# Two sums of quarters on GpSimd at each change of the resident operand, and row sums of the mixing's weights in fp32r

## The chip, the cores and the metric

The kernel runs on one core of a Trainium2 chip. The metric is its device time in microseconds; lower is better. TensorE (PE, with its weight loads as PEld) multiplies matrices, VectorE (DVE), ScalarE (ACT) and GpSimd (POOL) work on elements, and SyncE (SP) issues most of the DMAs. Operands lie in SBUF, products are accumulated in PSUM.

## The reference, cut to what matters

The program is one layer of a gated block over 1024 positions of 1024 channels, in fp32: a normalised input is projected into many parts; a windowed attention and a spatial gating are multiplied by gates and projected, and the two are added with further gates and projected once more.

```python
proj = h @ w_in[l]
q, k, v, za, u, vs, zs, gm = jnp.split(proj, IN_SPLITS, axis=-1)
...
a = (a * jax.nn.silu(za)) @ w_att_out[l]
sgo = chunked_spatial_gating(...)
sgo = (sgo * jax.nn.silu(zs)) @ w_sg_out[l]
ga, gs = jnp.split(jax.nn.sigmoid(gm + b_merge[l]), N_BRANCHES, axis=-1)
y = ga * a + gs * sgo
x = x + y @ w_o[l]
```

The spatial gating normalises `vs` over its channels with a scale `ln_g` and an offset `ln_b`, and mixes the 128 positions of a block by a masked 128 x 128 matrix per group of channels:

```python
v = layernorm(v, ln_g, ln_b)
...
mixed = jnp.einsum('gij,bnjgc->bnigc', w, vb) + jnp.transpose(b_s)[None, None, :, :, None]
return u * mixed.reshape(B, S, SG_WIDTH)
```

Since the offset is the same at all positions, it enters the mixed value as `ln_b` times the sum of a row of the mixing matrix. These are the row sums of the change.

## The kernel before, in words

**Products.** Every large product runs transposed, with one operand resident in SBUF (`b`) and the weights streaming past it. It is done by Strassen's scheme in Winograd's form: both operands are cut into quarters, and seven products of sums of quarters take the place of eight. The seven forms of the resident operand are `b11, t1, t2, b21, t3, b22, t4` (FORMS): b11, b21 and b22 are quarters themselves, t1 = q12 - q11 up to sign, t2 = t1 and q22 together, t3 = q11 combined with that, and t4 = q21 combined with it. Each of them lies in one buffer (tiles `T_b11h`, `T_b11l` and so on), so the form of a new operand can be written only after the old operand's last product has read it.

**Two halves of a number.** An fp32 number is split (`split`, L145 to 154) into a rounded high part, a cast on ScalarE (L153), and the rest, a subtraction on VectorE (L154). A product (`product`, L339) then is three passes (high by high, high by low, low by high) over four blocks of 128: 12 matmuls of 128 x 512. Weights are split likewise into `wh` and `wl`, each with three buffers of 128 x 1024; `split_next` does the next unit. `gemm_pair` runs the seven products of a pair of blocks of weights, and joins them by VectorE operations with one operand in PSUM (L369, L374, L378); its `finish` applies what follows, and sends the result to DRAM.

**Changes of the resident operand.** Two stages change it while the last pair of the stage before still runs: `s_forms` ahead of the projection of the gating branch (about 670 to 710 us) and `a_forms` ahead of that of the attention (about 746 to 790 us). `forms_of` gets the four quarters in `bq` tiles (128 x 2048 fp32, in halves of 128 x 1024), and forms sums in place by `combine` (L181 to 183, two instructions each): q12 := q11 - q12, then q12 := q22 + q12, then q11 := q12 - q11, and last q21 := q12 - q21. Between them each form is split into its tiles by `fill`. What leaves the pairs meanwhile is put into `a_dr` (L455, first change) and `y_dr` (second change) by DMAs that GpSimd issues.

**The mixing.** The second half of the projection `vs` runs as an ordinary gemm with eight PSUM banks as accumulators (L564, results into `xh` by L695 on ScalarE). Then the pairs of `u` begin. Their hooks run the statistics, the normalisation (L737), and, at the first and third pair (m = 0 and 4), `bias_of`: it loads a bias, makes the row sums of four groups of the mixing's weights `mix_w` (tile `wT`) by one fp32 matmul with a tile of `ones` (L747) into a bank `sc`, and combines the three on VectorE. `mix` uses these afterwards (L767). The `sc` banks have no other use in that stage.

**Order.** The instructions of an engine run in the order in which a scheduler put them when the program was built, and an instruction waits for the semaphores of what it reads and overwrites; so an instruction that moves in the source, or to another engine, also moves others against each other on the engines' queues.

Of the kernel before, what the change touches and what calls it, by code (L numbers as in the profile page):

```python
# [24 lines left out]
F32 = mybir.dt.float32  # L25
F32R = mybir.dt.float32r
AF = mybir.ActivationFunctionType
ALU = mybir.AluOpType
PSUM = bass.MemoryType.PSUM

P = 128
D = 1024
S = 1024
KC = D // P
# [18 lines left out]
def hybrid_tile(  # L53
# [16 lines left out]
    nc = tc.nc  # L70
# [8 lines left out]
    def nm(s):  # L79
        count[0] += 1  # L80
        return f"{s}_{count[0]}"

    def bank(tag, dt=F32):
        return psum.tile([P, 512], dt, name=nm("ps_" + tag), tag="ps_" + tag, bufs=2)

    def mtile(shape, dt, tag, bufs, pool=None):
        return (pool or main).tile(shape, dt, name=nm(tag), tag=tag, bufs=bufs)
# [13 lines left out]
    ident = const.tile([P, P], F32, name="ident")  # L101
# [10 lines left out]
    lb_sb = const.tile([P, KC], F32, name="lb_sb")  # L112
# [33 lines left out]
    def split(hi, lo, src, minus=False):  # L146
        if minus:
            nc.scalar.mul(hi, src, -1.0)
            nc.vector.scalar_tensor_tensor(
                lo, src, -1.0, hi.bitcast(F32), op0=ALU.mult, op1=ALU.subtract  # L150
            )
        else:
            nc.scalar.copy(hi, src)  # L153
            return nc.vector.tensor_sub(lo, src, hi.bitcast(F32))  # L154
# [18 lines left out]
    def new_b(names=FORMS):  # L173
        return {n: (slot(n + "h"), slot(n + "l")) for n in names}

    def fill_b(b, name, src, minus=None):
        hi, lo = b[name]
        for c in range(0, 4, 2):
            split(hi[:, c : c + 2, :], lo[:, c : c + 2, :], src[:, c : c + 2, :], name == "t2" if minus is None else minus)

    def combine(op, dst, a, c):  # L181
        for i in range(0, 4, 2):
            op(dst[:, i : i + 2, :], a[:, i : i + 2, :], c[:, i : i + 2, :])
# [22 lines left out]
    def split_next():  # L206

        if not units:
            begin_job()
        if not units:  # L210
            return
        halves, keys = units.pop(0)
        if keys[0][1] == 2:
            make_sums()
        hi = mtile([P, D], F32R, "wh", 3)
        lo = mtile([P, D], F32R, "wl", 3)
        if isinstance(halves, list):
            for c, half in enumerate(halves):
                split(hi[:, half_of(c)], lo[:, half_of(c)], half)
        else:  # L220
            wide = halves.shape[1]
            first = split(hi[:, 0:wide], lo[:, 0:wide], halves)
            if keys[0] == (done[0] - 1, 6) and done[0] > LAST_OF_Q + 2:
                make_sums(first)
        for c, key in enumerate(keys):
            ready[key] = hi[:, half_of(c)], lo[:, half_of(c)]
        if len(units) == 1:
            begin_job()

    def half_of(half):  # L230
        return slice(half * HALF, (half + 1) * HALF)
# [243 lines left out]

    outer = ExitStack()
    gelu = outer.enter_context(tc.tile_pool(name="gelu", bufs=1))
    head = ExitStack()
    hpool = head.enter_context(tc.tile_pool(name="head", bufs=1))
    xh = mtile([P, NT, D], F32, "xh", 1, gelu)  # L480
    stats = mtile([P, NT, 2, 6], F32, "bn", 1, gelu)
    mv = mtile([P, NT, 2], F32, "mv", 1, gelu)

    def htile(shape, dt, tag):
        return mtile(shape, dt, tag, 1, hpool)

    def load_x(t):
        xt = raw_tile()
# [145 lines left out]
    def gelu_of(t):  # L634
        two = xh[:, t : t + 2, 0:HALF]
        after(nc.scalar.activation(two, two, AF.Gelu), casts[-1])
        for i in range(2):
            statistics(t + i, 0)
# [6 lines left out]
    def make_forms():  # L645
# [29 lines left out]
        for c in range(0, 4, 2):  # L675
            form("t4", last[c // 2][:], c)
            yield

    accs = [bank(tag) for tag in ("mm", "mm", "o", "o", "sc", "sc", "tp", "tp")]
    aside = [lambda t=t: gelu_of(t) for t in range(0, NT, 2)]  # L680
    forms = make_forms()
# [3 lines left out]
    for c in range(4):  # L685
        if c + 2 < 4:
            weights.append(vs_weights(c + 2))
        for t in range(NT):
            wh, wl = weights[c]
# [7 lines left out]
                aside.pop(0)()  # L697
    while aside:
        aside.pop(0)()
    of_head = sinks.rearrange("(c e r) -> e c r", e=2, r=2)  # L700
    for e in range(2):
        nc.sync.dma_start(
# [5 lines left out]
    nc.sync.dma_start(lb_sb[:], ln_b)  # L708
    for _ in range(3):
        split_next()  # L710
    head.close()


    stage = ExitStack()
    stage.enter_context(outer)
    pool = stage.enter_context(tc.tile_pool(name="mixing", bufs=1))
    late = []

    def hook():
        for _ in range(2):  # L720
            if late:
                late.pop(0)()

    mix_w = mtile([P, KC, P], F32, "wT", 1, pool)
    nc.sync.dma_start(mix_w[:], sg_w)
    nc.vector.memset(mix_w[64:128, :, 0:64], 0.0)
    ones = mtile([P, P], F32, "ones", 1, pool)
    nc.gpsimd.memset(ones[:], 1.0)

    def statistics_of(t):  # L730
        statistics(t, 1)
# [9 lines left out]
    def bias_of(half):  # L741

        wT = mix_w[:, half * 4 : half * 4 + 4, :]
        bg = mtile([P, 4, P], F32, "bias", 1, pool)
        nc.sync.dma_start(bg[:].rearrange("p g i -> p (g i)"), sg_b[half_of(half)].partition_broadcast(P))
        rs = bank("sc")
        nc.tensor.matmul(  # L747
            rs[:],
            ones[:],
            wT.rearrange("p g i -> p (g i)"),  # L750
            start=True,
            stop=True,
        )
        for gg in range(4):
            g = half * 4 + gg
            nc.vector.scalar_tensor_tensor(
                bg[:, gg, :], rs[:, gg * P : (gg + 1) * P], lb_sb[:, g : g + 1], bg[:, gg, :], op0=ALU.mult, op1=ALU.add
            )
        return bg, wT

# [31 lines left out]
    for m in range(0, KC, 2):  # L792

        def finish(i, half, q, src, sign, m=m):
            nc.scalar.activation(q[:], src, AF.Gelu, scale=sign)
            late.append(lambda: mix(m + i, half, q))

        if m % 4 == 0:
            late.append(lambda m=m: bias.append(bias_of(m // 4)))
        gemm_pair(hb, finish, both)  # L800
# [5 lines left out]
    stage = ExitStack()  # L806
    pool = stage.enter_context(tc.tile_pool(name="keys", bufs=1))
# [43 lines left out]
    stage = ExitStack()  # L851
    pool = stage.enter_context(tc.tile_pool(name="queries", bufs=1))
# [229 lines left out]
    stage = ExitStack()  # L1082
    pool = stage.enter_context(tc.tile_pool(name="attention", bufs=1))
# [188 lines left out]
    stage = ExitStack()  # L1272
    pool = stage.enter_context(tc.tile_pool(name="later", bufs=1))
# [48 lines left out]
    def forms_of(qs):  # L1322
        q11, q12, q21, q22 = (qs[k] for k in QUARTERS)
        b = {}

        def fill(name, q):
            b.update(new_b((name,)))
            fill_b(b, name, q)

        combine(nc.vector.tensor_sub, q12, q11, q12)  # L1330
        yield
        fill("b11", q11)
        fill("t1", q12)
        combine(nc.vector.tensor_add, q12, q22, q12)
        fill("t2", q12)
        fill("b21", q21)
        combine(nc.vector.tensor_sub, q11, q12, q11)
        fill("t3", q11)
        fill("b22", q22)
        combine(nc.vector.tensor_sub, q21, q12, q21)  # L1340
        fill("t4", q21)
        yield b

# [8 lines left out]
    for m in range(0, KC, 2):  # L1352
        if m == 0:
            want_gates(at_dr, m)
        if m == 2:
            s_q = {}
            ahead_of_time += loads_of_quarters(s_q, s_dr)
        if m == 6:
            s_forms = forms_of(s_q)
            next(s_forms)  # L1360

        def finish(i, half, q, src, sign):
            nc.scalar.activation(q[:], src, AF.Silu, scale=sign)
            nc.vector.tensor_mul(q[:], q[:], gates.pop(0)[:])
            put(a_dr, m + i, half, q[:], nc.gpsimd)
            if m < 6:
                gates.append(get(at_dr, m + 2 + i, half, 4))

        gemm_pair(hb, finish, part_of_loads, "tp")
# [19 lines left out]
    for m in range(0, KC, 2):  # L1389
        if m == 2:  # L1390
            a_q = {}
            ahead_of_time += loads_of_quarters(a_q, a_dr)
        if m == 6:
            a_forms = forms_of(a_q)
            next(a_forms)

        def finish(i, half, q, src, sign):
            gated(q, src, sign, gate_of(gs_dr, m, i, half, KC))
            put(y_dr, m + i, half, q[:], nc.gpsimd)
            gates.append(get(gs_dr, m + 2 + i, half, 4) if m < 6 else get(ga_dr, i, half, 4))  # L1400

        gemm_pair(sb_, finish, part_of_loads, "tp")
# [125 lines left out]
    for p in range(4):  # L1528
        n, t, acc, x11 = N_PAIRS + p, T_ORDER[p], accs[p], firsts[p]
# [173 lines left out]
```

## Time and profile before

| | |
|---|---|
| time, median of 3 runs | 928.03 us (928.03 to 928.74) |
| the profiled execution's own time | 928.07 us |
| its span | 926.3 us |
| granted TensorE clock, mean | 0.997 |
| core | 1 of 1 |

The page gives for each engine the busy time and its share of the span. An instruction's idle time is put down to what released it. In the timeline, a row has the start, the duration, the engine, the line of the kernel, the operation, out<-in by tile names, the shape, and a count where equal neighbours are put together; behind it in brackets the idle time before it with its releaser. Neighbouring instructions of an engine overlap a little, so what an instruction costs its engine is the distance between starts. Matmuls recorded as 0.39 long start every 0.227 us.

### The profile page before, as it was taken

Reading aid. Unit: us, or ns where it says so; the run is one execution under the profiler, and the core shown is the slowest. Engines: PE = TensorE matmul, PEld = TensorE weight load, DVE = VectorE, ACT = ScalarE, POOL = GpSimd, SP = SyncE. Lnnn points to the kernel's source line nnn. Section 1 sums busy time; section 2 is a strip of 40 time slices with the busy share of each in tenths; the row PEclk is TensorE's granted clock in tenths of the full one; section 3 lists DMA queues with packets and bytes.
Section 4 is the critical chain, followed back from the end, with each engine's and each line's share of the span. In section 5 each row is a group of like instructions: output and inputs, shape, how many; then the busy total and the mean of one; then the engine's idle time right before and its main releaser. Section 6 shows DMA issues by size and latency. Waiting matters only on the chain.

```text
span 926.3 us, 13222 instructions
## 1 busy us (share of the span) xinstructions
PE 906.1 (98%) x4337; PEld 751.3 (81%) x4337; DVE 690.2 (75%) x1243; ACT 530.2 (57%) x1056; POOL 126.8 (14%) x189
## 2 busy tenths in 40 slices
PE   8999999999999989999999999999999999999996
PEld 5888888888888778778888888888887887888885
DVE  6874776656678678888878888746498589579996
ACT  7852433334444468887766676744475475467443
POOL 0002222213011001101111121001100111210012
PEclk9999999999999999999999999999999999999998
DMA  7328778887788777778787779779669765998632
GB/s 261 137 89 210 215 195 180 157 161 219 240 286 262 216 242 200 214 212 232 188 228 258 234 168 262 209 263 324 212 197 330 257 196 157 289 316 283 207 114 114
DMA packets 128972, 202.23 MB, mean 218 GB/s; under 512 B 12456, under 2 KB 60840, under 8 KB 128904
## 3 DMA queue, kind: packets, MB, share of 16 engines
q1 hardware_dynamic: 109752, 148.69, 49.1%
q0 software_dynamic: 19008, 52.44, 24.0%
q8 instruction: 34, 0.56, 0.2%
q14 instruction: 34, 0.28, 0.1%
q10 hardware_dynamic: 144, 0.26, 0.1%
HBM read 144.59 MB, written 86.11 MB: 249 GB/s over the span
## 4 chain that ended last, share of the span: by engine, by line
PE 74%; DVE 11%; DMA 7%; ACT 3%; issue 3%; SPq 1%; DVEq 0%; ACTq 0%
PE ps_mm L339 31%; PE ps_o L339 22%; PE ps_mm L595 4%; DVE wl L154 3%; PE ps_sc L339 2%; PE ps_tp L339 2%; PE ps_sc L1110 2%; PE ps_o L1195 2%; PE ps_tp L1154 2%; DMA wr<-in_w_dram 1%; PE ps_tp L564 1%; PE ps_sc L564 1%; PE ps_o L564 1%; PE ps_mm L564 1%; PE ps_tp L767 1%
## 5 line engine op out<-in xcount | busy, mean ns | idle before, releaser
L153 ACT CAST wh<-s 128x1024 fp32r<-128x1024 f32 (+1 forms) x78 | 78.2, 1005 | 95.3 <-PE ps_mm L339 44.7
L154 DVE TENSOR_TENSOR wl<-wr,wh 128x1024 fp32r<-128x1024 f32 (+1 forms) x80 | 75.7, 947 | 56.4 <-ACT wh L153 55.5
L153 ACT CAST wh<-wr 128x1024 fp32r<-128x1024 f32 (+1 forms) x80 | 66.3, 830 | 79.8 <-PE ps_mm L339 37.8
L154 DVE TENSOR_TENSOR wl<-s,wh 128x1024 fp32r<-128x1024 f32 (+1 forms) x78 | 90.9, 1166 | 12.1 <-ACT wh L153 12.1
L339 PE MATMUL ps_o<-T_b22h,wh 128*128 128x512 f32 x148 | 58.8, 398 | 1.7 <-ACT x L361 1.7
L339 PE MATMUL ps_o<-T_t1h,wh 128*128 128x512 f32 x148 | 59.2, 400 | 0.3 <-ACT wh L153 0.2
L339 PE MATMUL ps_o<-T_b22l,wh 128*128 128x512 f32 x148 | 57.8, 391 | 0.0
L339 PE MATMUL ps_o<-T_b22h,wl 128*128 128x512 f32 x148 | 57.8, 390 | 0.0
L339 PE MATMUL ps_o<-T_t1h,wl 128*128 128x512 f32 x148 | 57.7, 390 | 0.0
L339 PE MATMUL ps_o<-T_t1l,wh 128*128 128x512 f32 x148 | 57.7, 390 | 0.0
L339 PE MATMUL ps_mm<-T_b11h,wl 128*128 128x512 f32 x140 | 54.8, 392 | 2.1 <-DVE wl L154 2.1
L339 PE MATMUL ps_mm<-T_t4h,wh 128*128 128x512 f32 x140 | 55.2, 394 | 1.5 <-DVE x L374 0.8
L339 PE MATMUL ps_mm<-T_t2h,wh 128*128 128x512 f32 x140 | 54.9, 392 | 1.3 <-ACT x L357 1.2
L339 PE MATMUL ps_mm<-T_t3h,wh 128*128 128x512 f32 x140 | 55.4, 396 | 0.2 <-ACT x L364 0.2
L1123 ACT ACTIVATE pr<-ps_sc,sm 128x192 f32<-128x192 f32 (+2 forms) x128 | 50.9, 409 | 8.1 <-DVE sm L1119 7.1
L339 PE MATMUL ps_mm<-T_b11h,wh 128*128 128x512 f32 x140 | 55.0, 393 | 0.0
L339 PE MATMUL ps_mm<-T_t4h,wl 128*128 128x512 f32 x140 | 54.7, 391 | 0.0
L339 PE MATMUL ps_mm<-T_t3h,wl 128*128 128x512 f32 x140 | 54.7, 390 | 0.0
L339 PE MATMUL ps_mm<-T_b11l,wh 128*128 128x512 f32 x140 | 54.6, 390 | 0.0
L339 PE MATMUL ps_mm<-T_t2h,wl 128*128 128x512 f32 x140 | 54.6, 390 | 0.0
L339 PE MATMUL ps_mm<-T_t4l,wh 128*128 128x512 f32 x140 | 54.5, 390 | 0.0
L339 PE MATMUL ps_mm<-T_t2l,wh 128*128 128x512 f32 x140 | 54.5, 390 | 0.0
(352 smaller groups left out, 2403.9 us busy)
## 6 DMA issues: line engine op xcount, KB each, us to landing
wr<-in_w_dram SPq DMA_DIRECT2D x86, 256.0 KB
sums<-in_w_dram POOLq DMA_DIRECT2D x20, 512.0 KB, 5.6
s<-sums SPq DMA_DIRECT2D x20, 512.0 KB
s_dr<-x SPq DMA_DIRECT2D x32, 256.0 KB
q_hl<-qhl SPq DMA_DIRECT2D x16, 512.0 KB
q<-q_hl SPq DMA_DIRECT2D x64, 128.0 KB
wr<-in_w_dram SPq DMA_DIRECT2D x14, 512.0 KB
y_dr<-x POOLq DMA_DIRECT2D x28, 256.0 KB, 6.6
```

Source lines behind the costliest of these rows:

```text
L153: nc.scalar.copy(hi, src)
L154: return nc.vector.tensor_sub(lo, src, hi.bitcast(F32))
L339: nc.tensor.matmul(acc, lt, rt, start=fresh and k == 0 and n == 0, stop=k == 3 and n == 2, skip_group_check=True,)
L564: mm = nc.tensor.matmul(acc, lt, rt, start=k == 0 and n == 0, stop=k == KC - 1 and n == 2)
L595: nc.tensor.matmul(acc[:], lt, rt, start=k == 0 and n == 0, stop=k == KC - 1 and n == 2)
L767: nc.tensor.matmul(pm[:, t * P : (t + 1) * P], xh[:, half * 4 + t, g * P : (g + 1) * P], bias[-1][1][:, g % 4, :], start=True, stop=True,)
L1110: nc.tensor.matmul(sc[:, i, k0:], q_of[:, c, i * P : (i + 1) * P], kt[:, f, k0:], start=f == 0, stop=f == 1,)
L1123: nc.scalar.activation(held_in[c, i], sc[:, i, lo:hi], AF.Exp, bias=nmax[:, c, i : i + 1], scale=-1.0, accum_out=sums[:, c, i : i + 1],)
L1154: nc.tensor.transpose(dst, pr[:, i, block * P : block * P + width], ident[:])
L1195: nc.tensor.matmul(po[:, cs], lt, rt, start=n == 0, stop=n == len(terms) - 1)
```

## The change

Both edits leave the results what they were. At each change of the resident operand, the two last sums of quarters (into q11 and into q21, two instructions of 128 x 1024 each) are made by GpSimd instead of VectorE. The row sums are made before the first pair of `u` and no longer inside the first and third: the mixing's weights are loaded and masked, and the ones made, before the second-half gemm of `vs`; the weights are split once into high and low part, in one of the three `wh`/`wl` buffers, and two fp32r matmuls per half, four in all, sum them up directly after the gemm. The two `sc` banks keep the sums until the third pair. The ones are made by VectorE from the identity instead of by a memset on GpSimd.

In the built program the order on the engines changes as follows. On GpSimd, at the first change the two q11 instructions stand ahead of the first of the four `a_dr` issues, and the q21 instructions between the later ones; at the second the q11 instructions stand ahead of the four `y_dr` issues of the last pair and the q21 ones behind them. VectorE's order becomes `T_b21l`, both halves of `T_t3l`, `T_b22l` and `T_t4l`, and then the `wl` of the next pair. On TensorE, the first change had a third to a half of the next pair's first products ahead of the product of t4; now the product of t4 stands first. SyncE issues the load of the mixing's weights behind the fourth load of x. VectorE's and ScalarE's instructions in the first 62 us are put in another order.

```diff
--- before.py
+++ after.py
@@ -475,14 +475,10 @@
 
     outer = ExitStack()
     gelu = outer.enter_context(tc.tile_pool(name="gelu", bufs=1))
-    head = ExitStack()
-    hpool = head.enter_context(tc.tile_pool(name="head", bufs=1))
+    pool = outer.enter_context(tc.tile_pool(name="mixing", bufs=1))
     xh = mtile([P, NT, D], F32, "xh", 1, gelu)
     stats = mtile([P, NT, 2, 6], F32, "bn", 1, gelu)
     mv = mtile([P, NT, 2], F32, "mv", 1, gelu)
-
-    def htile(shape, dt, tag):
-        return mtile(shape, dt, tag, 1, hpool)
 
     def load_x(t):
         xt = raw_tile()
@@ -676,6 +672,11 @@
             form("t4", last[c // 2][:], c)
             yield
 
+    mix_w = mtile([P, KC, P], F32, "wT", 1, pool)
+    nc.sync.dma_start(mix_w[:], sg_w)
+    nc.vector.memset(mix_w[64:128, :, 0:64], 0.0)
+    ones = mtile([P, P], F32R, "ones", 1, pool)
+    nc.vector.tensor_scalar(ones[:], ident[:], 0.0, 1.0, op0=ALU.mult, op1=ALU.add)
     accs = [bank(tag) for tag in ("mm", "mm", "o", "o", "sc", "sc", "tp", "tp")]
     aside = [lambda t=t: gelu_of(t) for t in range(0, NT, 2)]
     forms = make_forms()
@@ -697,6 +698,13 @@
                 aside.pop(0)()
     while aside:
         aside.pop(0)()
+
+    row_sums = [bank("sc") for half in range(2)]
+    wh, wl = mtile([P, D], F32R, "wh", 3), mtile([P, D], F32R, "wl", 3)
+    split(wh[:], wl[:], mix_w[:].rearrange("p g i -> p (g i)"))
+    for half in range(2):
+        for n, part in enumerate((wh, wl)):
+            nc.tensor.matmul(row_sums[half][:], ones[:], part[:, half_of(half)], start=n == 0, stop=n == 1)
     of_head = sinks.rearrange("(c e r) -> e c r", e=2, r=2)
     for e in range(2):
         nc.sync.dma_start(
@@ -708,24 +716,16 @@
     nc.sync.dma_start(lb_sb[:], ln_b)
     for _ in range(3):
         split_next()
-    head.close()
 
 
     stage = ExitStack()
     stage.enter_context(outer)
-    pool = stage.enter_context(tc.tile_pool(name="mixing", bufs=1))
     late = []
 
     def hook():
         for _ in range(2):
             if late:
                 late.pop(0)()
-
-    mix_w = mtile([P, KC, P], F32, "wT", 1, pool)
-    nc.sync.dma_start(mix_w[:], sg_w)
-    nc.vector.memset(mix_w[64:128, :, 0:64], 0.0)
-    ones = mtile([P, P], F32, "ones", 1, pool)
-    nc.gpsimd.memset(ones[:], 1.0)
 
     def statistics_of(t):
         statistics(t, 1)
@@ -743,18 +743,10 @@
         wT = mix_w[:, half * 4 : half * 4 + 4, :]
         bg = mtile([P, 4, P], F32, "bias", 1, pool)
         nc.sync.dma_start(bg[:].rearrange("p g i -> p (g i)"), sg_b[half_of(half)].partition_broadcast(P))
-        rs = bank("sc")
-        nc.tensor.matmul(
-            rs[:],
-            ones[:],
-            wT.rearrange("p g i -> p (g i)"),
-            start=True,
-            stop=True,
-        )
         for gg in range(4):
             g = half * 4 + gg
             nc.vector.scalar_tensor_tensor(
-                bg[:, gg, :], rs[:, gg * P : (gg + 1) * P], lb_sb[:, g : g + 1], bg[:, gg, :], op0=ALU.mult, op1=ALU.add
+                bg[:, gg, :], row_sums[half][:, gg * P : (gg + 1) * P], lb_sb[:, g : g + 1], bg[:, gg, :], op0=ALU.mult, op1=ALU.add
             )
         return bg, wT
 
@@ -1334,10 +1326,11 @@
         combine(nc.vector.tensor_add, q12, q22, q12)
         fill("t2", q12)
         fill("b21", q21)
-        combine(nc.vector.tensor_sub, q11, q12, q11)
+
+        combine(nc.gpsimd.tensor_sub, q11, q12, q11)
         fill("t3", q11)
         fill("b22", q22)
-        combine(nc.vector.tensor_sub, q21, q12, q21)
+        combine(nc.gpsimd.tensor_sub, q21, q12, q21)
         fill("t4", q21)
         yield b
 
```

## The prediction

> **What bounds the kernel now.** I began with the page's totals and its chain of waits: they say which engine sets the end.
>
> ```profile
> span 926.3 us, 13222 instructions
> PE 906.1 (98%) x4337; PEld 751.3 (81%) x4337; DVE 690.2 (75%) x1243; ACT 530.2 (57%) x1056; POOL 126.8 (14%) x189
> PE 74%; DVE 11%; DMA 7%; ACT 3%; issue 3%; SPq 1%; DVEq 0%; ACTq 0%
> ```
>
> TensorE is busy for 98% of 926.3 us. The median is 928.03 and the profiled execution took 928.07, so 1.8 us lie around the span and the sums below can be set against 928.0 as they stand. Only two kinds of edit can move this time: fewer or shorter TensorE instructions, or less of TensorE's 20.2 us of idleness (926.3 - 906.1). The busy time by stretch says where idleness meets the change. Columns: length, then busy time and count of PE, PEld, DVE, ACT, POOL, then the granted clock, DMA share and GB/s.
>
> ```profile
> 20.00:62.00 42.00, 41.52 (x205) 33.90 (x204) 32.26 (x65) 31.05 (x55) 0.00 (x0) 1.00 0.38 131
> 62.00:106.00 44.00, 44.00 (x195) 36.43 (x195) 26.98 (x36) 15.45 (x19) 9.74 (x15) 1.00 0.72 194
> 690.00:725.00 35.00, 33.83 (x148) 27.39 (x147) 29.67 (x34) 19.14 (x25) 3.67 (x7) 1.00 0.94 331
> 768.00:802.00 34.00, 32.83 (x144) 26.37 (x143) 28.67 (x34) 17.66 (x24) 4.81 (x6) 1.00 0.69 210
> ...
> 690.00:695.00 5.00, 5.00 (x24) 4.14 (x23) 5.00 (x5) 2.48 (x3) 0.43 (x1) 1.00 0.92 264
> ...
> 705.00:710.00 5.00, 4.38 (x19) 3.65 (x20) 5.00 (x8) 0.20 (x1) 1.62 (x3) 1.00 1.04 395
> ```
>
> Both changes of the resident operand show idleness (33.83 of 35, 32.83 of 34), at a granted clock of 1.00. In steps of 5 us VectorE is busy 5.00 of 5.00 in all four steps from 690 to 710 (first and last shown): there VectorE is the engine that runs behind. GpSimd's little busy time there is issuing of DMAs. The timeline shows what TensorE loses.
>
> ```profile
> 699.92 0.39 PE L339 MATMUL ps_o<-T_b22h,wh 128*128 128x512 f32 x1
> ...
> 702.64 0.39 PE L339 MATMUL ps_mm<-T_b11h,wh 128*128 128x512 f32 x1
> ...
> 703.94 0.50 PE L339 MATMUL ps_o<-T_t1h,wh 128*128 128x512 f32 x1 [0.23 <-ACT wh L153]
> ...
> 705.62 0.50 PE L339 MATMUL ps_mm<-T_b11h,wl 128*128 128x512 f32 x1 [0.95 <-DVE wl L154]
> ...
> 709.83 0.39 PE L339 MATMUL ps_mm<-T_b11h,wl 128*128 128x512 f32 x1
> ...
> 783.52 0.50 PE L339 MATMUL ps_mm<-T_b11h,wl 128*128 128x512 f32 x1 [1.11 <-DVE wl L154]
> ```
>
> A product is 12 matmuls in 2.72 us (699.92 to 702.64), 0.227 each. From 702.64 to 709.83 there are 24, which need 5.44: the first change loses 7.19 - 5.44 = **1.75 us**, waiting for a `wl` that VectorE makes late. The second waits at the same place and loses about as much. So 3.5 us are the most that the four sums moved at each change can give back.
>
> **The change part by part.** *Row sums.* Each fp32 matmul (one per half) stood between two products:
>
> ```profile
> 119.84 0.39 PE L339 MATMUL ps_mm<-T_t3h,wl 128*128 128x512 f32 x1
> 120.07 1.02 PE L747 MATMUL ps_sc<-wT,ones 128*128 128x512 f32 x2
> ...
> 121.15 0.40 PE L339 MATMUL ps_o<-T_b22l,wh 128*128 128x512 f32 x1
> ```
>
> From 119.84 to 121.15 are 1.31 us, with two ordinary steps in them (0.45), so one fp32 matmul costs 0.86 and both 1.72. Four fp32r matmuls at 0.227 take 0.91. Gain: **0.81 us**. They now stand between the second-half gemm of vs, whose stretch (62 to 106) has no idleness, and the first pair. Their operand is split long before. What may be late is the split of the pair's second unit, since the mixing's split takes one of its three `wh`/`wl` buffers:
>
> ```profile
> 106.24 0.39 PE L564 MATMUL ps_tp<-wh,T_b22l 128*128 128x512 f32 x1
> 106.46 0.39 PE L339 MATMUL ps_mm<-T_b11h,wh 128*128 128x512 f32 x1
> ...
> 107.16 1.04 ACT L153 CAST wh<-s 128x1024 fp32r<-128x1024 f32 x1
> ...
> 108.35 1.22 DVE L154 TENSOR_TENSOR wl<-s,wh 128x1024 fp32r<-128x1024 f32 x1
> ...
> 109.64 0.39 PE L339 MATMUL ps_o<-T_t1h,wl 128*128 128x512 f32 x1
> ```
>
> The gemm's last matmul (106.24) and the pair's first stand without a gap. The split is already made this late, and ready at 109.57. Its reader moves from 109.64 to 110.55 behind the row sums, so 0.98 us are spare; with no cover the cost would be about one split, 2.2. I take 0. The load of the mixing's weights, their memset and the `ones` move into the first 62 us, where VectorE and SyncE's queue take another order. TensorE's idleness there (42.00 - 41.52) limits a gain to 0.5; for a loss I take one VectorE operation of 128x1024, 1.1. Value 0.
>
> *The four sums of each change.* VectorE's timeline of the first, and GpSimd's only comparable operations (from the view grouped by line):
>
> ```profile
> 679.10 1.22 DVE L183 TENSOR_TENSOR bq<-bq,bq 128x1024 f32<-128x1024 f32 x1
> ...
> 690.65 1.22 DVE L154 TENSOR_TENSOR T_b21l<-bq,T_b21h 128x1024 fp32r<-128x1024 f32 x1
> 691.79 2.35 DVE L183 TENSOR_TENSOR bq<-bq,bq 128x1024 f32<-128x1024 f32 x2
> 694.06 1.21 DVE L154 TENSOR_TENSOR T_b22l<-bq,T_b22h 128x1024 fp32r<-128x1024 f32 x1
> ...
> 698.61 2.35 DVE L183 TENSOR_TENSOR bq<-bq,bq 128x1024 f32<-128x1024 f32 x2
> 700.88 0.68 DVE L154 TENSOR_TENSOR wl<-wr,wh 128x512 fp32r<-128x512 f32 x1
> 701.48 2.35 DVE L154 TENSOR_TENSOR T_t4l<-bq,T_t4h 128x1024 fp32r<-128x1024 f32 x2
> 703.75 0.68 DVE L369 TENSOR_TENSOR x<-x,ps_tp 128x512 f32<-128x512 f32 x1
> 704.35 1.22 DVE L154 TENSOR_TENSOR wl<-wr,wh 128x1024 fp32r<-128x1024 f32 x1
> ...
> L1546 POOL TENSOR_TENSOR g<-bq,bq 128x512 f32<-128x512 f32 x2 | 2.6, 1305 | 4.3 <-DVE bq L1541 3.9 <-issue 0.4
> L582 POOL TENSOR_TENSOR T_t1l<-T_t3h,T_t1h 128x512 fp32r<-128x512 f32 x1 | 1.3, 1282 | 7.6 <-ACT T_t1h L581 7.6
> L832 POOL CAST vt<-vt 128x512 fp32r<-128x512 f32 x2 | 1.2, 622 | 0.0
> ```
>
> Two sums take VectorE 2.27 us (691.79 to 694.06), so four free 4.54. GpSimd needs 1.28 to 1.31 for 128x512; the 128x1024 form is not in the trace. Bounds: 2 x 1.28 = 2.56 if all of it grows with size, about 2.0 if as much as the whole 0.62 of a 128x512 cast did not. I take 2.45. Four take 9.8 us, one after another.
>
> If the two engines ran side by side, that length would be covered: q12, which all of it reads, is done at about 680.2, two sums then end by 685.2 and the others, which must wait until `T_b21l` has been subtracted from q21 (691.8, with both halves before the sums as in the old order), by 696.7; then come the casts and `T_t4l`. The new order puts the last product, which reads t4, directly at 702.64. GpSimd's own queue holds four issues of `a_dr` at the first change and four of `y_dr` at the second behind the sums; what reads them comes a stage later. In that case both stalls go, 3.0 to 3.5.
>
> They may not run side by side. Nearly every VectorE operation here reads two operands from SBUF (the `wl`, `T_*l` and sums), as GpSimd's would. The trace has one close meeting of such a pair:
>
> ```profile
> 914.57 0.69 DVE L1580 TENSOR_TENSOR bq<-bq,g 128x512 f32<-128x512 f32 x1
> ...
> 915.08 1.33 POOL L1546 TENSOR_TENSOR g<-bq,bq 128x512 f32<-128x512 f32 x1 [3.92 <-DVE bq L1541]
> ...
> 915.96 0.69 DVE L1541 TENSOR_TENSOR bq<-bq,ps_o 128x512 f32<-128x512 f32 x1 [0.32 <-PE ps_o L339]
> ...
> 916.78 1.28 POOL L1546 TENSOR_TENSOR g<-bq,bq 128x512 f32<-128x512 f32 x1 [0.38 <-issue]
> ```
>
> The second L1546 starts 0.13 after the L1541 that makes its operand ends (916.65). The first starts 0.43 after its own L1541 (it ends just ahead, at 914.65), while the two-input L1580 ran from 914.57 to 915.26: 0.3 us more, and it begins about when L1580's operands have been read. One meeting is weak, but points to GpSimd waiting for VectorE. The Trainium skill ("SBUF — State Buffer", section "Who interferes with whom") says outright that a VectorE instruction with two SBUF inputs contends with a GpSimd one that reads SBUF, and that whoever issues first holds the shared pair for its whole length. The 0.3 us agree with it; by it the sums below come out longer.
>
> Under such **mutual exclusion** VectorE's saturated stretch has 9.8 us of blockage in place of 4.54 of its own work: 5.3 us more, less what it can still do meanwhile, operations with an operand in PSUM such as L369 (0.60). I laid the new order of the four engines out by these durations, with products of 2.72 us, casts of 0.95 and each wait the program states; the same layout of the old order gives 1.5 us of stall, where the trace has 1.75. With GpSimd winning each contest, TensorE waits 1.4 us at the next pair's t1 (a late `wl`), 0.45 at b21, 2.0 at t3, 0.9 at t4 and 1.0 in the pair behind: 5.75, a net **+4.2**. With VectorE winning, GpSimd starves between back-to-back subtractions, t4 comes 4.6 late, and with 0.8, 0.8, 0.6 and 2.0 elsewhere it is 8.8, net +7.3. The second change lays out to +3.2 and +4.0. With sums of 2.0 us each all four shrink: 2.6 and 5.75, 1.6 and 2.4. So exclusion costs 4.2 (2.6 + 1.6) to 11.3 (7.3 + 4.0). I take GpSimd winning at 2.45: 4.2 + 3.2, and 0.2 for the 0.05 by which 2.45 exceeds the 2.4 laid out, **+7.6**.
>
> Sum: 928.0 - 0.8 + 0 + 0 + 7.6 = 934.8; I say **934.8**, a loss, within 930.3 to 939.6 on its own (4.2 and 11.3, with the 1.1 above).
>
> **The rivals.** *Side by side* (GpSimd's sums are free) is the case on the other side: 928.0 - 3.5 - 0.8 = 923.7, or 924.2 with 3.0. For it: GpSimd is 14% busy and the lengths fit as shown. Against it: the delayed L1546, and no row in which a VectorE operation with two SBUF inputs runs all through a GpSimd one. It decides once each of the eight sums costs TensorE less than 0.54 us (3.5 + 0.8 over 8); the exclusion above charges 1.4 (7.6 + 3.5 over 8).
>
> *Partial contention*: each sum holds VectorE only as long as one of its own did, so the 4.54 us are not freed and TensorE waits for `wl` about as now. The row sums remain: 927.2; or 929.0, when t4's earlier place in the order costs one 0.9 stall per change. Nothing in the trace speaks for a part rather than all or none.
>
> *A late start of the first pair*, with both engines free: the split at 107.16 loses its 0.98 of cover if its buffer frees later than that. At the full 2.2, and the first 62 us at +1.1, it takes back 3.3 of the 4.3 gained: 927.0. Against it: the buffers were last read at 106.2, when the second-half gemm ended.
>
> *The change doesn't do what it says*: the first pair waits where the row sums were, so their 0.8 isn't gained. With exclusion that is 935.6; TensorE's uninterrupted start at 106.5 speaks against it.
>
> **How the numbers follow.** Exclusion 0.62, exclusion without the row sums' gain 0.03, side by side 0.24, partial 0.08, a late start 0.03. A change of under 0.2% (1.9 us) cannot be told from none here. Faster: 0.24, the partial case's and the late start's share below 926.2, 0.03, together 0.27. Same: the rest of these two, 0.08. Slower: 0.65. The range reaches past 934.8 to 939.0, which leaves out VectorE winning every contest at 2.45 us, and down to 923.5, which takes in the side-by-side case.
>
> **What would show it.** Under exclusion: L183's lines on GpSimd well over 2.5 us long or starting late, VectorE's rows at 677 to 705 stretched or parted by gaps of 2 us without a releaser, and TensorE's waits naming `T_t4l`, `T_t3l` and `wl`; PE busy in 690 to 725 falls below 33.8. Side by side: VectorE has idle time in 690 to 705, both 0.95 and 1.11 waits are gone, and busy PE equals the stretch. Right for the row sums: four matmuls 0.227 apart at 106.5, and none at 120 and 155. The prediction fails if GpSimd's sums leave VectorE's durations as they are.

## The result, and the profile after

| | before | after |
|---|---|---|
| median of 4 runs | 928.03 us (927.27 to 928.74) | 943.83 us (939.96 to 949.82) |
| profiled execution, span | 926.3 us | 948.0 us |
| ratio of the times | | 1.0167, 95% interval 1.0136 to 1.0198 |

The changed kernel is slower by 1.4% to 2.0%. Its four runs are 10 us apart, those of the kernel before 1.5; the profiled execution is the slowest of the four (949.82). From the page of the changed kernel, the totals, and from its view of busy time by stretch, the two changes of the resident operand and two stretches of 2 us (columns as before):

```profile
span 948.0 us, 13234 instructions
PE 913.3 (96%) x4337; PEld 757.1 (80%) x4337; DVE 699.5 (74%) x1237; ACT 530.7 (56%) x1057; POOL 155.8 (16%) x196
...
690.00:725.00 35.00, 27.98 (x113) 22.57 (x113) 27.26 (x28) 17.15 (x22) 16.21 (x9) 0.88 0.69 234
768.00:802.00 34.00, 29.05 (x109) 22.93 (x108) 32.49 (x26) 20.25 (x26) 13.80 (x8) 0.85 0.35 120
...
688.00:690.00 2.00, 2.00 (x5) 1.60 (x6) 2.00 (x2) 2.00 (x3) 0.17 (x1) 0.55 0.73 244
...
704.00:706.00 2.00, 0.52 (x1) 0.50 (x2) 1.02 (x1) 1.93 (x3) 1.98 (x3) 0.50 0.46 170
```

TensorE is busy for 27.98 of 35 us in the first change, where it was 33.83, and its granted clock, 1.00 before, is 0.88 and 0.85 over the changes, about 0.5 just after long waits. The loss is located by the first matmul of a pair, which both traces have. First the kernel before, then the changed one, from their timelines of TensorE:

```profile
667.28 0.39 PE L339 MATMUL ps_mm<-T_b11h,wh 128*128 128x512 f32 x1
...
726.15 0.39 PE L339 MATMUL ps_mm<-T_b11h,wh 128*128 128x512 f32 x1
...
804.18 0.39 PE L339 MATMUL ps_mm<-T_b11h,wh 128*128 128x512 f32 x1
```

```profile
668.39 0.39 PE L339 MATMUL ps_mm<-T_b11h,wh 128*128 128x512 f32 x1
...
739.29 0.39 PE L339 MATMUL ps_mm<-T_b11h,wh 128*128 128x512 f32 x1
...
825.38 0.39 PE L339 MATMUL ps_mm<-T_b11h,wh 128*128 128x512 f32 x1
```

Up to the first change the changed kernel is 1.1 us late. The stretch with the first change takes 70.90 us where it took 58.87 (**+12.0**), that with the second 86.09 where it took 78.03 (**+8.1**), and 0.5 comes behind: 21.7, the difference of the spans. What happens at the first change stands in the timelines of VectorE, GpSimd, ScalarE and TensorE of the changed kernel:

```profile
679.61 0.68 DVE L369 TENSOR_TENSOR x<-x,ps_tp 128x512 f32<-128x512 f32 x1
680.21 3.20 DVE L183 TENSOR_TENSOR bq<-bq,bq 128x1024 f32<-128x1024 f32 x1
...
684.47 2.85 DVE L1357 TENSOR_TENSOR x<-x,g 128x512 f32<-128x512 f32 x1
687.24 0.67 DVE L374 TENSOR_TENSOR x<-x,ps_mm 128x512 f32<-128x512 f32 x1
...
693.58 1.28 DVE L1357 TENSOR_TENSOR x<-x,g 128x512 f32<-128x512 f32 x2
...
699.33 2.34 DVE L154 TENSOR_TENSOR T_b22l<-bq,T_b22h 128x1024 fp32r<-128x1024 f32 x2
...
679.92 2.41 POOL L183 TENSOR_TENSOR bq<-bq,bq 128x1024 f32<-128x1024 f32 x1 [7.76 <-DVE bq L183]
683.56 3.21 POOL L183 TENSOR_TENSOR bq<-bq,bq 128x1024 f32<-128x1024 f32 x1 [1.23 <-DVE bq L183]
...
693.79 10.07 POOL L183 TENSOR_TENSOR bq<-bq,bq 128x1024 f32<-128x1024 f32 x1 [2.17 <-ACT x L1356]
...
704.93 2.37 POOL L183 TENSOR_TENSOR bq<-bq,bq 128x1024 f32<-128x1024 f32 x1
...
703.90 1.04 ACT L153 CAST T_t4h<-bq 128x1024 fp32r<-128x1024 f32 x1 [7.86 <-POOL bq L183]
704.85 0.58 ACT L357 COPY x<-ps_mm 128x512 f32<-128x512 f32 x1
...
687.97 0.62 PE L339 MATMUL ps_mm<-T_t4h,wh 128*128 128x512 f32 x1 [3.10 <-DVE x L374]
...
692.41 0.39 PE L339 MATMUL ps_mm<-T_b11h,wh 128*128 128x512 f32 x1
...
705.49 0.80 PE L339 MATMUL ps_mm<-T_t2h,wh 128*128 128x512 f32 x1 [7.02 <-ACT x L357]
...
709.81 0.40 PE L339 MATMUL ps_tp<-T_b21h,wl 128*128 128x512 f32 x1
```

Read along the clock. While GpSimd makes a sum (679.92 to 682.33), a VectorE sum with two SBUF operands takes 3.20 us in place of 1.22, ending 1 us after it; then L1357 takes 2.85 in place of 0.68. L369, which has one operand in PSUM, keeps its 0.68 beside the first sum. L374 stands behind the blocked L1357, and TensorE's next product, the last of the old operand, waits 3.10 us for it. The third GpSimd sum takes 10.07 us: it ends 2.2 us after VectorE's last subtraction ahead of a wait, which ends at 701.7. The cast of `T_t4h` on ScalarE waits 7.86 us for that sum, the copy L357 stands behind the cast, and TensorE waits 7.02 us for the copy, because its next product accumulates in the bank that L357 reads. After each wait the 12 matmuls of a product take 4.44 us (687.97 to 692.41) and 4.32 (705.49 to 709.81) in place of 2.72. 3.10 + 1.72 + 7.02 + 1.60 = 13.4, less the 1.75 that before lost here: 11.7 of the 12.0.

The row sums, in TensorE's timeline of the changed kernel:

```profile
106.40 0.39 PE L560 MATMUL ps_tp<-wh,T_b22l 128*128 128x512 f32 x1
106.63 0.39 PE L707 MATMUL ps_sc<-wh,ones 128*128 128x512 f32 x1
...
107.33 0.39 PE L707 MATMUL ps_sc<-wl,ones 128*128 128x512 f32 x1
107.56 0.39 PE L339 MATMUL ps_mm<-T_b11h,wh 128*128 128x512 f32 x1
```

Four matmuls in 0.93 us, with nothing idle before or behind them.

### The profile page after: what moved, and what is told of

The parts are those of the page before. It is cut to its first block, busy times and chain, and to the rows that moved or that the text cites. A ratio compares the mean times of both kernels' runs of the same rounds, so it can differ in the third digit from the quotient of the medians.

```text
span 948.0 us, 13234 instructions
## 1 busy us (share of the span) xinstructions
PE 913.3 (96%) x4337; PEld 757.1 (80%) x4337; DVE 699.5 (74%) x1237; ACT 530.7 (56%) x1057; POOL 155.8 (16%) x196
## 4 chain that ended last, share of the span: by engine, by line
PE 80%; DVE 7%; DMA 5%; issue 4%; ACT 3%; POOL 2%; SPq 0%; ACTq 0%; DVEq 0%; POOLq 0%
PE ps_mm L339 34%; PE ps_o L339 25%; PE ps_mm L591 4%; PE ps_sc L1102 3%; PE ps_tp L339 2%; PE ps_o L1187 2%; PE ps_tp L1146 2%; PE ps_sc L339 2%; POOL bq L183 2%; DVE wl L154 2%; PE ps_tp L759 2%; PE ps_tp L560 1%; PE ps_sc L560 1%; PE ps_o L560 1%; PE ps_mm L560 1%
## 5 line engine op out<-in xcount | busy, mean ns | idle before, releaser
L154 DVE TENSOR_TENSOR wl<-wr,wh 128x1024 fp32r<-128x1024 f32 (+1 forms) x80 | 77.8, 974 | 66.0 <-ACT wh L153 65.2
L339 PE MATMUL ps_mm<-T_t3l,wh 128*128 128x512 f32 x140 | 55.2, 394 | 0.0
```

Of the source, the lines that this page charges most:

```text
L339: nc.tensor.matmul(acc, lt, rt, start=fresh and k == 0 and n == 0, stop=k == 3 and n == 2, skip_group_check=True,)
```

## The experiments

For each kernel, the table has the time beside that of the kernel before in the same comparison, and how much longer than before the stretches with the two changes are, measured between the same first matmuls as above in its one profile (58.87 and 78.03 us before).

| run | time, us | before, us | ratio (95%) | change 1 | change 2 |
|---|---|---|---|---|---|
| e1_rowsum | 928.64 | 929.12 | 1.0001 (0.9988 to 1.0014) | 0.0 | -0.1 |
| e2_q11 | 934.54 | 929.12 | 1.0069 (1.0055 to 1.0084) | +2.5 | +3.3 |
| e3_q21 | 941.56 | 929.12 | 1.0149 (1.0131 to 1.0167) | +8.3 | +5.1 |
| e4_cast2 | 943.57 | 929.12 | 1.0166 (1.0149 to 1.0183) | +6.6 | +7.2 |
| f1_after | 946.27 | 928.14 | 1.0194 (1.0172 to 1.0216) | +6.6 | +6.8 |
| f2_read | 938.81 | 928.14 | 1.0109 (1.0096 to 1.0122) | +5.0 | +5.3 |
| f3_write | 927.49 | 928.14 | 0.9993 (0.9983 to 1.0003) | 0.0 | -0.1 |
| f4_busy | 944.83 | 928.14 | 1.0180 (1.0165 to 1.0195) | +9.4 | +5.8 |
| g1_q21_cast | 939.97 | 928.88 | 1.0117 (1.0104 to 1.0130) | +6.4 | +3.8 |
| g2_order | 925.90 | 928.88 | 0.9966 (0.9953 to 0.9978) | -1.7 | -1.9 |
| g3_order_rowsum | 924.65 | 928.88 | 0.9946 (0.9933 to 0.9959) | -1.7 | -1.8 |

**The parts of the change, one at a time.** e1 is the changed kernel with both sums back on VectorE; e2 (first diff) and e3 (second) are the kernel before with one sum moved.

```diff
-        combine(nc.vector.tensor_sub, q11, q12, q11)
+        combine(nc.gpsimd.tensor_sub, q11, q12, q11)
```

```diff
-        combine(nc.vector.tensor_sub, q21, q12, q21)
+        combine(nc.gpsimd.tensor_sub, q21, q12, q21)
```

> Only the row sums' part of the change; all sums of quarters on VectorE as before. If the loss comes from the two engines excluding each other, this keeps the gain seen ahead of 300 us (1.0 us) and loses nothing at the changes of the resident operand: 926.5 to 927.5 us, both waits for wl of 0.95 and 1.11 still there. Rival, the row sums' part itself costs time (banks held, a later split, the 2.2 us lost between 300 and 346 us): 929 to 931.

> Kernel before, with only the two q11 sums of each change on GpSimd. Exclusion: each VectorE operation with two SBUF operands that meets one of them is stretched from 1.2 to about 3 us, TensorE waits about 3 us for the operation at L374 and then runs at half clock for some us: 4 to 6 us per change, 934 to 940 in all. Rival, only the late t4 matters: 926 to 929.

> Kernel before, with only the two q21 sums of each change on GpSimd. Exclusion with VectorE winning: the first of them takes 7 to 10 us at the first change, T_t4h waits for it, the copy at L357 behind that cast, and TensorE for the copy: 5 to 9 us at the first change and 1 to 4 at the second, 934 to 940. Rival, only the stretched VectorE operations matter: under 931.

The row sums' part neither wins nor loses a time that can be told from none: 928.64 lies between the expected 926.5 to 927.5 and the rival's 929 to 931. The two sums lose 5.8 (2.5 + 3.3) and 13.4 us in the profiles, 19.2 together, beside the 20.1 of both in the execution above and 13.4 in f1's. By the medians they lose 5.4 and 12.4, 17.9 together, beside 15.8 and, in f1, 18.1: the loss is theirs. TensorE's timeline of e2, with its stretches by clock, shows two equal waits with unequal consequences:

```profile
687.47 0.50 PE L339 MATMUL ps_mm<-T_t4h,wh 128*128 128x512 f32 x1 [3.10 <-DVE x L374]
...
767.89 0.62 PE L339 MATMUL ps_mm<-T_t4h,wh 128*128 128x512 f32 x1 [3.12 <-DVE x L374]
...
688.00:692.00 4.00, 4.00 (x19) 3.26 (x18) 4.00 (x6) 4.00 (x7) 0.55 (x1) 1.00 0.49 164
...
768.00:772.00 4.00, 4.00 (x11) 3.16 (x12) 3.91 (x5) 1.14 (x2) 0.55 (x1) 0.57 0.49 173
```

After 3.10 us the clock stayed at 1.00 and 19 matmuls fell into 4 us; after 3.12 it was 0.57 and 11 did. In e3 the casts of `T_t4h`, which wait for GpSimd, stand ahead of other work on ScalarE. Its timeline, and TensorE's first wait:

```profile
696.49 1.04 ACT L153 CAST T_t4h<-bq 128x1024 fp32r<-128x1024 f32 x1 [7.73 <-POOL bq L183]
...
700.86 1.99 ACT L153 CAST T_t3h<-bq 128x1024 fp32r<-128x1024 f32 x2
702.76 0.58 ACT L364 COPY x<-ps_mm 128x512 f32<-128x512 f32 x1
...
703.38 0.80 PE L339 MATMUL ps_mm<-T_t3h,wh 128*128 128x512 f32 x1 [7.09 <-ACT x L364]
```

t3 doesn't depend on GpSimd in this kernel, but its casts come behind those of t4, and TensorE waits 7.09 us for the copy behind them all.

**The same kernel again, and ScalarE's queue.** f1 is the changed kernel unaltered. e4 and g1 make the form of t4 in a hook of the first new pair (behind its second or third product) and put its casts behind the copy just issued, e4 in the changed kernel, g1 in e3:

```diff
         combine(nc.gpsimd.tensor_sub, q21, q12, q21)
-        fill("t4", q21)
         yield b
+        b.update(new_b(("t4",)))
+        for c in range(0, 4, 2):
+            hi, lo = (v[:, c : c + 2, :] for v in b["t4"])
+            after(nc.scalar.copy(hi, q21[:, c : c + 2, :]), pace[0])
+            nc.vector.tensor_sub(lo, q21[:, c : c + 2, :], hi.bitcast(F32))
+        yield b
```

> The changed kernel once more, for the spread of its time and a second profile. If the clock drops after each wait of about 3 us by chance (one of two equal waits of 3.10 and 3.12 us in the q11 kernel was followed by a slow clock), times spread over about 8 us, 938 to 950, and a faster run's profile has the same waits with fewer slow matmuls. Rival, GpSimd's starvation varies: its longest sum (10.07 us) is then shorter in a faster run.

> The changed kernel, with the two casts of T_t4h put behind the copies L357 and L361 of the new operand's first products on ScalarE's queue. If the 7 us come from the queue (copy behind a cast that waits for GpSimd), that wait and the slow clock after it go: 8 to 10 us less than the changed kernel, 933 to 937. If they come from t4 itself being late, the wait only moves to the product of t4 and the time stays at 940 to 945.

> The kernel with only the q21 sums on GpSimd, and the casts of T_t4h ordered behind the first new pair's copies L357, L361 and L364 on ScalarE (T_t3h ahead of them too). The first GpSimd sum still waits for a gap in VectorE's subtractions. If the 7.09 and 5.10 us come from ScalarE's queue, they go, VectorE reaches T_t4l at about 699, GpSimd's sums then take 4.9 us, and TensorE waits 2 to 4.5 us for a later wl or t4: 931 to 936. If they come from the late sum alone, the whole wait moves to the product of t4: 939 to 943.

f1's profiled execution took 940.86 us (its six runs go up to 950.21). GpSimd's and VectorE's timelines at the place where the other execution had 10.07 us, and all of TensorE's waits at the first change:

```profile
691.64 2.73 POOL L183 TENSOR_TENSOR bq<-bq,bq 128x1024 f32<-128x1024 f32 x1 [2.17 <-ACT x L1356]
...
691.43 3.50 DVE L1357 TENSOR_TENSOR x<-x,g 128x512 f32<-128x512 f32 x2
...
685.82 0.50 PE L339 MATMUL ps_mm<-T_t4h,wh 128*128 128x512 f32 x1 [3.10 <-DVE x L374]
...
702.72 0.50 PE L339 MATMUL ps_mm<-T_t3h,wh 128*128 128x512 f32 x1 [1.36 <-ACT x L364]
...
709.79 0.50 PE L339 MATMUL ps_mm<-T_t4h,wh 128*128 128x512 f32 x1 [1.33 <-DVE x L374]
```

Here GpSimd gets in between the two operations at L1357, and the second is held up; in the execution of 949.82, with the same 0.21 us between the starts (693.58 and 693.79), VectorE's second went first, and GpSimd waited on for as long as VectorE had subtractions to do. The program is the same: who wins is open from run to run. The wait of 7.02 us for L357 is gone, and the first change is 5.4 us shorter (12.0 against 6.6). Not all of the spread is this: at the second change GpSimd's sums go the same way in both executions, and 1.3 us lie between them (8.1 against 6.8), where matmuls ran slowly for longer.

That spoils e4. Its profile also shows GpSimd winning (2.73 us), so its smaller loss at the first change cannot be put down to the casts: f1, without them, loses the same 6.6. Its median is 943.57, f1's in another comparison 946.27, the first one's 943.83. The 933 to 937 expected of e4 did not come, and it decides nothing on the case in which VectorE wins. g1 does better, since e3's first sum was starved in each profile of that order (8.99 us; 9.00 in f4). GpSimd's timeline of g1 and TensorE's:

```profile
689.52 13.01 POOL L183 TENSOR_TENSOR bq<-bq,bq 128x1024 f32<-128x1024 f32 x1 [2.17 <-DMA g<-gs_dr]
...
710.05 0.79 PE L339 MATMUL ps_mm<-T_b11h,wh 128*128 128x512 f32 x1 [6.26 <-ACT wh L153]
```

The 7.09 us ahead of t3 are gone, as the queue's part; but VectorE, no longer held up itself, starves GpSimd for 13.01 us, and what now stands behind the casts on ScalarE is a `wh` cast, for which TensorE waits 6.26. The order of the queue is worth 3.2 us of 13.4 by the profiles (e3 less g1) and 1.4 of 12.4 by the medians; most of the loss is the late sum, as the rival had it. Since that sum also became later, the two causes are not cleanly parted.

**What it is that collides.** f2 and f3 leave all sums of the kernel before on VectorE, and give GpSimd work that nobody waits for, overwriting q22 after its last use, f2 as in the first diff, f3 as in the second:

```diff
         fill("b22", q22)
+        combine(nc.gpsimd.tensor_sub, q22, q12, q22)
```

```diff
         fill("b22", q22)
+        for v in range(5):
+            nc.gpsimd.memset(q22[:, 2 * (v % 2) : 2 * (v % 2) + 2, :], float(v))
```

> Kernel before, all its own sums on VectorE, and in addition GpSimd overwrites q22 by q12 - q22 after its last use (two instructions of 128x1024 per change that nobody waits for). Exclusion: VectorE's subtractions that meet them take about 3 us, and the stall of 1.75 us grows by 2 to 5 us per change: 932 to 939. Rival, only waiting for GpSimd's results costs: 928 to 930.

> As the run before, but in place of the two sums GpSimd fills q22 five times per change with a constant (about as long, writing only). If what collides is the reading of operands, no VectorE operation is stretched and the time is that of the kernel before, 928 to 930; if any GpSimd operation on SBUF collides, as the run before.

GpSimd's and VectorE's timelines of f2, and TensorE's longest wait at its first change:

```profile
695.90 13.95 POOL L183 TENSOR_TENSOR bq<-bq,bq 128x1024 f32<-128x1024 f32 x2 [4.98 <-DMA s<-sums]
...
704.23 0.68 DVE L369 TENSOR_TENSOR x<-x,ps_tp 128x512 f32<-128x512 f32 x1
704.83 2.78 DVE L154 TENSOR_TENSOR wl<-wr,wh 128x1024 fp32r<-128x1024 f32 x1
707.54 2.86 DVE L1387 TENSOR_TENSOR x<-x,g 128x512 f32<-128x512 f32 x1
710.32 0.68 DVE L374 TENSOR_TENSOR x<-x,ps_mm 128x512 f32<-128x512 f32 x1
...
707.67 0.50 PE L339 MATMUL ps_mm<-T_b11h,wl 128*128 128x512 f32 x1 [2.51 <-DVE wl L154]
```

and of f3:

```profile
696.62 2.99 POOL L1341 MEMSET bq<- 128x1024 f32 x3 [4.95 <-DMA s<-sums]
...
699.84 2.35 DVE L183 TENSOR_TENSOR bq<-bq,bq 128x1024 f32<-128x1024 f32 x2
```

In f2 the first sum waits 8 us through all of VectorE's operations with two SBUF operands, and begins when L369, which has one in PSUM, runs. Then `wl` takes 2.78 us, and at the next boundary the second sum is first and L1387 takes 2.86. With nobody waiting for GpSimd the kernel is 1.1% slower: TensorE waits 2.51 us for that `wl`. In f3 the same engine writes the same tile for 5 us at the same place and VectorE's rows keep their lengths: what collides is an operation that reads, not one that only writes.

**The clock.**

> The kernel with only the q21 sums on GpSimd, and 18 further matmuls (4.1 us at full clock, into a bank nobody reads) ahead of the product of t3 in the first pair of each new operand, where TensorE waited 7.09 and 5.10 us. If a long wait lowers the clock, the matmuls behind it stay at 0.227 us and 2 to 4 us come off: 937 to 940. If the slow clock has another cause, the time stays at 941 to 943 or rises.

f4 adds 18 `nc.tensor.matmul` calls of 128x512 on `T_b21h` to e3, into a bank `sc`. TensorE's timeline of f4:

```profile
704.56 0.50 PE L339 MATMUL ps_mm<-T_t3h,wh 128*128 128x512 f32 x1 [3.07 <-ACT x L364]
...
713.69 0.47 PE L339 MATMUL ps_mm<-T_t4h,wh 128*128 128x512 f32 x1 [1.80 <-DVE x L374]
```

The idle wait shrank from 7.09 to 3.07 us, but the kernel got no faster: 1.0180 of before against e3's 1.0149. A wait of 1.80 us for L374 that e3 doesn't have stands behind: TensorE was ready earlier than VectorE. Behind the 3.07 us the 12 matmuls of a product still took 4.46. At the second change the wait shrank from 5.10 to 1.03 us and the product took 2.86, and yet that stretch got no shorter (+5.8 against +5.1), with 2.06 us of waiting for L374. The added matmuls also moved the next pair's first matmuls behind the product of t4, so the run doesn't isolate the clock. How much of the slow clock would have been waiting anyway stays open.

**A better order.** The stall of the kernel before was a `wl` behind the subtractions of `T_t4l`. g2 is the kernel before with the form of t4 made in the hook behind the product of t3, its subtractions ordered behind L374; g3 adds the row sums' part.

```diff
         combine(nc.vector.tensor_sub, q21, q12, q21)
-        fill("t4", q21)
         yield b
+        b.update(new_b(("t4",)))
+        for c in range(0, 4, 2):
+            hi, lo = (v[:, c : c + 2, :] for v in b["t4"])
+            nc.scalar.copy(hi, q21[:, c : c + 2, :])
+            after(nc.vector.tensor_sub(lo, q21[:, c : c + 2, :], hi.bitcast(F32)), term[0])
+        yield b
```

> Kernel before, all sums on VectorE, with only VectorE's order changed at both changes: the subtractions of T_t4l stand behind the operation that joins the product of t3 (L374), and so behind the wl that TensorE waited 0.95 and 1.11 us for. If the stall of 1.75 us is a matter of order, 0.5 to 1 us of it is left per change: 926.0 to 927.3. If VectorE's load decides, the wait moves to the product of t4: 927.5 to 929.

> The run before together with the row sums' part. If the two gains add: 925 to 926.5, below both the kernel before and the changed one. If the row sums' gain is lost again between 300 and 346 us, where TensorE waits after late DMAs: as the run before.

The two stretches of g2 by busy time:

```profile
690.00:725.00 35.00, 35.00 (x156) 28.85 (x155) 31.14 (x35) 19.76 (x26) 4.05 (x8) 1.00 0.91 330
768.00:802.00 34.00, 34.00 (x151) 28.14 (x151) 29.83 (x36) 19.03 (x25) 6.32 (x8) 1.00 0.78 230
```

TensorE has no idleness left at either change: the whole stall, 1.7 and 1.9 us, was a matter of VectorE's order, with its work unchanged. g2 is faster than before by 0.2% to 0.5%, g3 by 0.4% to 0.7%; g3 has the best median, 924.65, though the intervals of the two overlap.

## Why the prediction was wrong in size

- **The direction and the cause held.** The forecast was a loss by mutual exclusion, at 934.8 with a range up to 939.0; the median is 943.83. The side-by-side case is out: 3.20 and 2.85 us in place of 1.22 and 0.68. The Trainium skill ("SBUF — State Buffer", section "Who interferes with whom") has a VectorE instruction with two SBUF inputs collide with a GpSimd one that reads SBUF, not with one that only writes it; f2 and f3 agree, with 2.78 and 2.86 us against unchanged rows.
- **GpSimd's length** was taken as 2.45 us; undisturbed ones took 2.37 and 2.41. Right.
- **Row sums.** 0.86 us each at the two old places was taken, and 0.91 for the four new: 0.93 in the trace, and the first pairs show no wait for the split whose buffer was taken. The gain of 0.8 is there in the traces for 300 us: the pair that starts at about 296 us starts at 296.0 to 296.4 in the five kernels with this part and at 296.8 to 297.4 in the eight without. It isn't seen in the time of e1, whose interval reaches from a gain of 1.1 us to a loss of 1.3; g3 is 1.25 us below g2. The stretch from that pair to the one at about 346 us takes 48.3 to 52.1 us in the five and 48.2 to 49.8 in the eight, enough to hide it; what lengthens it was not tested.
- **The stall of 1.75 us** does go, as the sum had it. But that it needed less work on VectorE was a wrong turn: g2 removes it by order alone.
- **The step that failed** is the layout of the four engines' order by "each wait the program states", in two of its terms. Its waits stand at t1, b21, t3 and t4, for `wl` and late forms; none is for the operations that must have read a PSUM bank before the next product is added into it (L374 on VectorE, L357 and L364 on ScalarE). The trace has TensorE's waits there: for L374 (3.10 us at each change, in the old operand's last pair) and for L357 (7.02), operations that need nothing of GpSimd but stand in a queue behind something that is held up by it. The layout also ran every matmul at 0.227 us and put a slower clock at nothing (the stretches that the prediction shows are all at 1.00); the two products behind the waits cost 3.3 us more in the first change alone. By TensorE's timelines, the 20.1 us of both changes are 12.8 of longer waits and 7.3 of matmuls further apart than 0.227; f1's 13.4 are 9.6 and 3.7.
- **The sizes by that.** GpSimd winning was laid out at +4.2 and +3.2; f1's profile has 6.6 and 6.8. VectorE winning was +7.3 at the first change; the first profile has 12.0. I forecast the first case, but the same program meets both. In f1 the waits of the first change add up to 5.79 us (3.10 + 1.36 + 1.33), beside 5.75 laid out. That is luck: the largest stands in the old operand's last pair, where the layout had none, and those ahead of t3 and t4 are for L364 and L374, not for late forms.
- **Of the signs listed**, L183 on GpSimd over 2.5 us, VectorE's stretched rows and busy TensorE under 33.8 came; that TensorE's waits would name `T_t4l`, `T_t3l` and `wl` did not.
- **A bound of the sum.** The lower one, 930.3, takes off 1.1 us for the first 62 us, where the text itself allows a gain of 0.5 at most; that gives 930.9. The forecast doesn't rest on it.

## What to carry to other kernels

An elementwise operation with two SBUF operands did not move to GpSimd for nothing here: beside a saturated VectorE it cost its whole length there, or waited until VectorE paused. Look first at what VectorE runs meanwhile. Where an engine's result comes later, list what stands behind its reader on each queue, and among that the reads of PSUM banks that a product is still to be added into: those, not the result's own consumers, stopped TensorE here. Before work is moved off a busy engine, try its order: the same VectorE work in another order gave back the whole stall.

## What the runs showed of the hardware that was not expected

- A waiting GpSimd sum isn't always served next: one that needs 2.4 us took 8.99 to 13.01 behind back-to-back VectorE operations, and began when one with an operand in PSUM ran, or VectorE waited. At an open boundary the same program went either way (10.07 and 2.73 us).
- The granted clock fell to 0.50 to 0.57 after waits of TensorE of 3.1 to 7.0 us, and matmuls took 0.43 us for some 3 us or more. It did not fall after each: the profiles of the changed kernel, f1, e4 and e2 have eight waits of 3.10 to 3.12 us, and the product behind one of them took 2.87 us, behind the others 4.00 to 5.28. It also fell behind a wait of 1.85 us (796 us in the changed kernel, a product of 4.42). The Trainium skill ("TensorE: Matmul & The Clock Gate", "Part 1: The HAM clock gate") gives an idle window of about 3.4 us for the drop. The drops after shorter waits here differ from that, and the measurement decides.
